# An encoder trunk whose input projection goes from 256 to 512 columns a step

## The chip, the cores and the metric

The kernel runs on one core of a Trainium2 chip. The metric is the device time of the whole program in microseconds (us): the median of three runs was 1551.15 us (1551.09 to 1554.43). All inputs and outputs are float32 in the chip's main memory.

## The reference, cut to what matters

There are two layers over 1024 tokens of width 1024. Each layer normalises its input, projects it with one weight matrix of 1024 x 3072, runs three groups of attention heads side by side, gates their outputs, projects them back and adds a normalised result to its input.

```python
for l in range(2):
    proj = rms_norm(x, pre_norm[l]) @ w_in[l]            # 1024 x 3072
    dq, dk, dv, dgate, gq, gk, gv, ggate, mq, mgate = split(proj,
        [384, 384, 384, 384, 384, 128, 128, 384, 256, 256])
    # 6 differential heads: (softmax(q1 k1) - lam * softmax(q2 k2)) v, rotary on q, k
    oa = rms_norm(diff_attention(rope(dq), rope(dk), dv, lam), subln) * silu(dgate)
    # 6 grouped-query heads on 2 kv heads, q and k normalised, axial rotary
    ob = gqa(axial(rms_norm(gq)), axial(rms_norm(gk)), gv) * silu(ggate)
    # 4 heads over 256 memory tokens
    mk, mv = split(rms_norm(mem, mem_norm[l]) @ w_mem_kv[l], 2)
    om = softmax(mq mk / 8) mv * silu(mgate)
    x = x + rms_norm(concat(oa, ob, om) @ w_out[l], post_norm[l])
```

## The kernel before, in words

**Precision.** Projections and scores are computed from float32 values split in two: a high half that TensorE takes in one pass and the rest as a low half. A product needs three matmuls (high x high, high x low, low x high). Line 493 issues them for the input projection, line 1394 for the output projection. For the products with the values, ScalarE writes the exponential (line 853) and its half-precision copy `eh` (line 857), GpSimd or VectorE the rest `el` (line 860), and lines 504 to 506 multiply both with the values.

**Input projection.** The 3072 columns are cut into 12 chunks of 256 (`dq0`, `dk0`, ... ; some join two pieces of 128 from different places), and the memory projection into two (`mk`, `mv`). For a chunk and a tile of 128 tokens, a *step* runs 8 blocks of rows x 3 products = 24 matmuls into half of a PSUM bank (`matmul_chunk`). Its weights come as four pieces of 256 rows x 256 columns (`load_piece`): a DMA into one of three raw buffers `rt`, the high half by ScalarE (line 392), the low half by VectorE or GpSimd (line 393 or 394), into one of eight places of the ring `wt`. A place is free again once the last tile's step has used it. After a step `post` takes the result out of PSUM: rotary and normalisation on VectorE and GpSimd (`rope_lin`, `rope_ax`), transposes on TensorE (line 662) and a store to a scratch tensor for query and key columns (`put_T`), a split of values (`put_v`), a tanh for gates (`put_gate`).

**Stages of a layer.** Chunks `dq0`, `dk0`, `dv0`, `mk`, `mv` run first, in PSUM tiles of two banks (kinds `s0`, `s1`). The nine others run in single banks (kind `st`) as filler of low priority beside differential attention: 12 half-heads, each of 16 maximum matmuls (line 1026, reduced by line 897) and eight units of scores (line 1036), each unit with its exponential. Every two units make one product with the values (`pv_part`). Then come the grouped-query heads (lines 1238, 1239, 1250, 1251) and the memory heads (1293, 1294), then the output projection and the norms, in which the next layer's input is normalised and its first weights are loaded.

**Order of the work.** Nothing is ordered by hand. A planner (`Plan`) simulates five engines, the DMA queue, PSUM banks (`Banks`, with a priority and a limit for each kind in `KINDS`) and rings of buffers, with a cost for each operation (`PE`, `ACT`, `DVE`, `POOL`, `LAT`), and every engine's instructions are issued in the order in which the plan starts them. All DMAs go through SP's queue. On the chip each queue then runs in that order, and waits where something is late.

Of the kernel before, what the change touches and what calls it, by code (L numbers as in the profile page):

```python
# [22 lines left out]
P = 128  # L23
# [11 lines left out]
DQ, DK, DV, DG, GQ, GK, GV, GG, MQ, MG = 0, 384, 768, 1152, 1536, 1920, 2048, 2176, 2560, 2816  # L35
CHUNKS = {
    "dq0": ((DQ, 256),),
    "dq1": ((DQ + 256, 128), (GK, 128)),
    "dk0": ((DK, 256),),
    "dk1": ((DK + 256, 128), (GV, 128)),  # L40
    "dv0": ((DV, 256),),
    "dv1": ((DV + 256, 128), (MQ, 128)),
    "dg0": ((DG, 256),),
    "dg1": ((DG + 256, 128), (MG, 128)),
    "gq0": ((GQ, 256),),
    "gq1": ((GQ + 256, 128), (MQ + 128, 128)),
    "gg0": ((GG, 256),),
    "gg1": ((GG + 256, 128), (MG + 128, 128)),
    "mk": ((0, 256),),
    "mv": ((256, 256),),  # L50
}
VCOLS = {"dv0": (0, 256), "dv1": (0, 128), "dk1": (128, 256), "mv": (0, 256)}
VKEY = {"dv0": "d0", "dv1": "d1", "dk1": "g", "mv": "m"}
# [21 lines left out]
DVE_FIX = 0.13  # L75
PV_N = 2
X_GATE, XT = 2, 4
DMA_RATE = 300.0
SLACK = 0.8

KINDS = {'un': (0.5, 2, 2), 'z': (1, 2, 2), 's0': (2, 2, 2), 's1': (0, 2, 2), 'st': (1, 4, 1), 'pv': (1, 1, 1), 'tr': (-1, 2, 1), 'mx': (2, 4, 1), 'zh': (3, 2, 1)}
# [6 lines left out]
class Event:  # L88
# [4 lines left out]
    def fire(self, plan):  # L93
        self.n -= 1
        if self.n == 0:
            for p in self.waiters:
                plan.push(plan.t, p, None)
            self.waiters = []

# [78 lines left out]
class Plan:  # L178
# [5 lines left out]
    def __init__(self):  # L184
        self.t = 0.0
        self.seq = 0
        self.heap = []
        self.busy = {k: False for k in self.LAT}
        self.queue = {k: [] for k in self.LAT}
        self.used = {k: 0.0 for k in self.LAT}  # L190
        self.until = {k: 0.0 for k in self.LAT}
        self.port = {"dve": 0.0, "pool": 0.0}
        self.live = 0
# [12 lines left out]
    def start(self, eng):  # L206
# [4 lines left out]
        self.used[eng] += dur  # L211
        if port:
            dur += max(0.0, self.port["pool" if eng == "dve" else "dve"] - self.t)
            self.port[eng] = self.t + dur
# [4 lines left out]
        self.push(self.t + dur + (self.LAT[eng] if lat is None else lat), proc, None)  # L219

    def advance(self, proc, val):
        gen, done = proc
        while True:
# [18 lines left out]
            if kind == "wait":  # L242
                if cmd[1].n > 0:
                    cmd[1].waiters.append(proc)
                    return
# [26 lines left out]
def trunk(ctx, tc, t_in, t_out):  # L272
# [80 lines left out]
    def pair(name, nb, n=S):  # L353
        return [dram.tile([P, nb, n], F32, name=f"{name}{i}") for i in range(2)]

    scr = {"dq0": pair("s_dqa", 2), "dq1": pair("s_dqb", 2), "dk0": pair("s_dka", 2), "dk1": pair("s_dkb", 1),
           "gq0": pair("s_gqa", 2), "gq1": pair("s_gqb", 2), "dv1": pair("s_mqa", 1), "mk": pair("s_mka", 2, NM)}


    def load_piece(src, j, cols, w, col, vmax, prio=0):  # L360

        ri = yield take("rt")
        rt = wr.tile([P, 2, NC], F32, name="rt")
        lst, off = [], 0
        for c0, n in cols:
            lst.append((rt[:, :, off:off + n],
                        src[j * 2 * P:(j + 1) * 2 * P, c0:c0 + n].rearrange("(a p) n -> p a n", p=P), n))
            off += n
        yield wait(dmas(lst, prio))
        if vmax is not None:  # L370
            v0, v1 = VCOLS[col]
            yield DVE(2 * (v1 - v0), lambda: dve.tensor_reduce(
                out=vmax[:, 1 + j:2 + j], in_=rt[:, :, v0:v1], axis=AX.XY, op=ALU.max, apply_absolute_value=True))
        hi, lo, wi = yield from split_w(rt)
# [4 lines left out]
    def split_w(rt, p2=None, name=None):  # L379
        if p2 == "big":  # L380
            wi = yield take("big")
            t = new_big()
            hi, lo = (t[:, h * 512:(h + 1) * 512].rearrange("p (a n) -> p a n", a=2) for h in range(2))
        elif p2 is None:
            wi = yield take("wt")
            hi = wp.tile([P, 2, NC], F32R, name="wt")
            lo = wp.tile([P, 2, NC], F32R, name="wt")
        else:
            wi = None
            hi = p2.tile([P, 2, NC], F32R, name=name + "h")  # L390
            lo = p2.tile([P, 2, NC], F32R, name=name + "l")
# [5 lines left out]
    def new_w():  # L397
        return {"t": [None] * 4, "ev": [Event() for _ in range(4)], "scale": Event()}

    def vscale(vmax, gmx, w, sc, key):  # L400
# [4 lines left out]
        yield DVE(4, lambda: dve.tensor_reduce(out=wm[:, 0:1], in_=vmax[:, 1:5], axis=AX.X, op=ALU.max))  # L405
# [77 lines left out]
    def matmul_chunk(ps, xhi, xlo, w, last, prio):  # L483

        for j in range(4):
# [14 lines left out]
    def attend(o, v, es):  # L500

        n = len(es)
        for kt, (eh, el) in enumerate(es):
            pe.matmul(o[:, 0:65], lhsT=eh, rhs=v[:, kt, 0:65], start=(kt == 0), stop=False, skip_group_check=True)  # L504
            pe.matmul(o[:, 0:64], lhsT=eh, rhs=v[:, kt, 66:130], start=False, stop=False, skip_group_check=True)  # L505
            pe.matmul(o[:, 0:65], lhsT=el, rhs=v[:, kt, 0:65], start=False, stop=(kt == n - 1),  # L506
                      skip_group_check=True)
# [4 lines left out]
    def make_layer(l):  # L512
# [4 lines left out]
        L.W = {c: new_w() for c in (*FIRST, *REST)}  # L517
# [5 lines left out]
        stored = {c: Event(NT if c != "mk" else 2) for c in scr}  # L523
        gate_ev = {c: Event(NT // 2) for c in ("dg0", "dg1", "gg0", "gg1")}
        vfull = {c: Event(NT if c != "mv" else 2) for c in VCOLS}
# [6 lines left out]
        opened = Event()  # L532
        attn_open = Event()


        def weights(chunks):
            for c in chunks:
                src = t_in["w_mem_kv"][l] if c in ("mk", "mv") else w_in
                vmax = None
                if c in VCOLS:  # L540
                    vmax = small.tile([P, 8], F32, name="gm")
                    pl.spawn(vscale(vmax, (lambda: mgm[0]) if c == "mv" else (lambda: L.gmx), L.W[c], sc, VKEY[c]))
                evs = []
                for j in range(4):
                    ev = Event()
                    pl.spawn(load_piece(src, j, CHUNKS[c], L.W[c], c, vmax, -7 if c == FIRST[0] else 0), ev)
                    evs.append(ev)
                yield wait(evs[1])
# [42 lines left out]
        def put_v(vt, ps, c, n, key):  # L591
# [3 lines left out]
            cv = sc[VKEY[c]]  # L595
# [4 lines left out]
            vfull[c].fire(pl)  # L600
# [55 lines left out]
        def put_T(nat, nb, c, t, ni):  # L656
# [3 lines left out]
            def f():  # L660
                for j in range(nb):
# [11 lines left out]
            yield wait(dmas([(scr[c][x][:, :nb, t * P:(t + 1) * P], raw(s)[:, :nb, :], 64 * nb)  # L673
                             for x, s in ((0, hi), (1, lo))]))
# [5 lines left out]
        def put_gate(ps, t, c, freed):  # L680
            k = yield take("sq")
            th = Q["pj"].tile([P, NC], F32, name="sq", bufs=SQ)
            yield ACT(NC, lambda: act.activation(th, ps, AF.Tanh, scale=0.5), POST, "p")
# [1107 lines left out]
```

## Time and profile before

| | |
|---|---|
| median of three runs | 1551.15 us |
| profiled execution, its own time | 1553.02 us |
| its span, first to last instruction | 1551.2 us |
| mean granted TensorE clock | 0.987 |
| TensorE busy, matmuls | 1487.1 us, 15920 instructions |
| VectorE, ScalarE, GpSimd busy | 1036.2, 896.5, 903.0 us |
| moved by DMA | 163.97 MB |

The span is what the profile covers; the execution's own time is 1.8 us longer. Busy time of TensorE includes the modelled tails of matmuls, which overlap; the mean of one matmul is for that reason longer than the distance from one to the next. A share of busy time is a mean over stages, so the tables of stages and the chain of waits are read beside it.

### The profile page before, as it was taken

The page shows a single profiled execution, that of the slowest core. Times are in us where ns is not written, and L with a number is a line of the kernel's source. Part 1 is how long each engine was busy: PE and PEld are TensorE (multiplying, and loading weights), DVE is VectorE, ACT ScalarE, POOL GpSimd, SP SyncE. Part 2 cuts the span into 40 slices and gives each one's busy share as a digit, 9 for nine tenths or more (in the row PEclk, how much of TensorE's full clock was granted, in tenths as well). Part 3 has the DMA queues.
Part 4 walks back from the last instruction along what each step waited for, and adds up shares of the span by engine and source line. Part 5 has one row for each costly group of instructions (what it writes and reads, how often), then busy time and mean ns, then how long its engine had stood idle before and what let it go on. Part 6 is the DMA issues. An engine that isn't in the chain of part 4 may idle for free. (4 is left out here: it accounts for less than half of the span.)

```text
span 1551.2 us, 39344 instructions
## 1 busy us (share of the span) xinstructions
PE 1487.1 (96%) x15920; PEld 1375.1 (89%) x15920; DVE 1036.2 (67%) x2042; ACT 896.5 (58%) x1428; POOL 903.0 (58%) x647
## 2 busy tenths in 40 slices
PE   6999999999999999999999999999999998899997
PEld 5999999989999888888889999999899998788886
DVE  7747776788865886825566487776887757777143
ACT  4332668767668576673333346677657657576511
POOL 4133668789768486561122257678887757585500
PEclk9999999999999998999999999999999999899999
DMA  6435223233323644215254523223332156332242
GB/s 203 134 106 152 77 77 103 71 96 94 95 82 84 175 117 100 57 49 199 94 163 133 137 83 97 80 59 103 111 104 63 56 144 174 79 84 70 83 147 95
DMA packets 166048, 163.97 MB, mean 106 GB/s; under 512 B 14853, under 2 KB 140357, under 8 KB 165866
## 3 DMA queue, kind: packets, MB, share of 16 engines
q1 hardware_dynamic: 165866, 161.46, 35.7%
q8 instruction: 125, 2.05, 0.6%
q14 instruction: 57, 0.47, 0.1%
HBM read 110.96 MB, written 50.09 MB: 104 GB/s over the span
## 5 line engine op out<-in xcount | busy, mean ns | idle before, releaser
L860 POOL TENSOR_TENSOR el<-e,eh 128x1024 f16<-128x1024 f32 x258 | 570.0, 2221 | 208.0 <-ACT eh L857 194.7
L897 DVE TENSOR_REDUCE mx<-ps 128x1 f32<-128x512 f32 (+1 forms) x608 | 404.6, 684 | 145.6 <-PE ps L1026 86.8
L493 PE MATMUL ps<-wt,big 128*128 128x256 f32 x3456 | 490.0, 285 | 2.0 <-DVE nat L606 1.7
L493 PEld LDWEIGHTS ps<-wt,big 128*128 128x128 f32 x3456 | 465.0, 190 | 18.8 <-ACT e L853 2.0
L853 ACT ACTIVATE e<-pp 128x1024 f32<-128x1024 f32 x304 | 309.3, 1024 | 108.2 <-PE pp L1251 61.9
L857 ACT ACTIVATE eh<-e 128x1024 f16<-128x1024 f32 x262 | 275.4, 1057 | 2.4
L504 PEld LDWEIGHTS <-eh 128*128 128x128 f16 x2144 | 195.0, 96 | 14.4 <-issue 10.9
L394 POOL TENSOR_TENSOR wt<-rt,wt 128x512 fp32r<-128x512 f32 x89 | 123.7, 1401 | 136.6 <-ACT wt L392 96.0
L506 PEld LDWEIGHTS <-el 128*128 128x128 f16 x2144 | 196.6, 99 | 3.8 <-POOL el L860 3.4
L505 PEld LDWEIGHTS <-eh 128*128 128x128 f16 x2144 | 196.6, 97 | 0.7 <-issue 0.5
L436 POOL TENSOR_SCALAR u<-ss 128x1 f32<-128x1 f32 (+3 forms) x96 | 23.9, 249 | 253.3 <-DVE ss L1478 109.0
L493 PE MATMUL pp<-wt,big 128*128 128x256 f32 x1152 | 156.5, 291 | 8.8 <-POOL wt L394 4.1
L1026 PE MATMUL ps<-sdk,sdq 96*128 96x512 f32 x384 | 158.2, 413 | 3.9 <-DVE mx L897 2.4
L493 PEld LDWEIGHTS pp<-wt,big 128*128 128x128 f32 x1152 | 144.6, 194 | 11.7 <-POOL wt L394 4.9
L504 PE MATMUL ps<-vd,eh 128*128 128x65 f16 x1536 | 150.3, 193 | 0.2
L505 PE MATMUL ps<-vd,eh 128*128 128x64 f16 x1536 | 149.5, 194 | 0.0
L506 PE MATMUL ps<-vd,el 128*128 128x65 f16 x1536 | 149.0, 192 | 0.0
L1036 PE MATMUL pp<-sdq,sdk 98*128 98x256 f32 x768 | 125.8, 286 | 0.0
L1036 PEld LDWEIGHTS pp<-sdq,sdk 98*128 98x128 f32 x768 | 112.5, 190 | 5.3
L1250 PE MATMUL pp<-big 128*128 128x256 f32 x384 | 102.6, 297 | 0.3 <-ACT e L853 0.3
L1251 PE MATMUL pp<-big 67*128 67x256 f32 x384 | 100.3, 291 | 1.5 <-DMA big<-nl 1.5
L949 ACT ACTIVATE o<-ps 128x130 f32<-128x130 f32 (+1 forms) x160 | 46.1, 288 | 92.7 <-PE ps L506 91.8
(243 smaller groups left out, 2829.4 us busy)
## 6 DMA issues: line engine op xcount, KB each, us to landing
rt<-in_w_in SPq DMA_DIRECT2D x48, 256.0 KB
rt<-in_w_in SPq DMA_DIRECT2D x96, 128.0 KB
gt<-g_scr SPq DMA_DIRECT2D x32, 256.0 KB
rt<-in_w_out SPq DMA_DIRECT2D x32, 256.0 KB
sdq<-s_dqa SPq DMA_DIRECT2D x48, 128.0 KB
sdk<-s_dka SPq DMA_DIRECT2D x48, 128.0 KB
big<-s_gqa SPq DMA_DIRECT2D x24, 256.0 KB
big<-s_gqb SPq DMA_DIRECT2D x24, 256.0 KB
```

What stands on the lines that cost most here:

```text
L394: (POOL(512, lambda: pool.tensor_sub(out=lo, in0=rt, in1=raw(hi))), W_BIAS[1]))
L493: pe.matmul(ps, lhsT=x[:, kt, :], rhs=y[:, a, :], start=(kt == 0 and n == 0), stop=(kt == KT - 1 and n == 2))
L504: pe.matmul(o[:, 0:65], lhsT=eh, rhs=v[:, kt, 0:65], start=(kt == 0), stop=False, skip_group_check=True)
L505: pe.matmul(o[:, 0:64], lhsT=eh, rhs=v[:, kt, 66:130], start=False, stop=False, skip_group_check=True)
L506: pe.matmul(o[:, 0:65], lhsT=el, rhs=v[:, kt, 0:65], start=False, stop=(kt == n - 1), skip_group_check=True)
L853: yield ACT(1024, lambda: act.activation(e, ps, AF.Exp, scale=scale), 0, "p")
L857: yield either((ACT(1024, lambda: act.activation(eh, e, AF.Copy)), 0.0), (DVE(1024, lambda: dve.tensor_copy(out=eh, in_=e), 0, fast=True, ...
L860: (POOL(1024, lambda: pool.tensor_sub(out=el, in0=e, in1=eh)), 0.0))
L897: yield DVE(512, lambda: dve.tensor_reduce(out=out_ap, in_=src, axis=AX.X, op=ALU.max), MXP[0])
L1026: yield (512, lambda ps, n=n: pe.matmul(ps, lhsT=q()[0:96, i * P:(i + 1) * P], rhs=k()[0:96, n * 512:(n + 1) * 512], start=True, stop=True ...
L1036: pe.matmul(ps[:, a * 256:(a + 1) * 256], lhsT=k()[0:98, kt * P:(kt + 1) * P], rhs=q()[0:98, j * 256:(j + 1) * 256], start=True, stop=True)
L1250: pe.matmul(o, lhsT=ka()[:, ks], rhs=a()[:, qs], start=True, stop=False)
```

## The change

The 12 chunks become six blocks A to F of 512 contiguous columns, and the two memory chunks become one block M. A step runs 24 matmuls of 512 columns into a whole bank. A piece of weights is now 128 rows x 512 columns, of the same size, and a block has eight. The ring keeps its eight places; six of M's pieces go to a memory pool of its own. Block A runs alone first, then B, C, D, F and E as filler and M beside them; a count of finished units limits how early a filler step may start. What is taken out of PSUM after a step is grouped anew, and scratch tensors are one for each of q, k and so on. A product with the values is issued in two steps: all high parts once the high halves are there, the low parts once the low halves are. The planner's costs get new figures and a model of TensorE's clock.

```diff
-CHUNKS = { "dq0": ((DQ, 256),), "dq1": ((DQ + 256, 128), (GK, 128)),
...
-FIRST = ("dq0", "dk0", "dv0", "mk", "mv")
-REST = ('dg0', 'dq1', 'dk1', 'dv1', 'gq1', 'gq0', 'dg1', 'gg1', 'gg0')
-W_SLOTS = 8
+BLOCKS = {"A": 0, "B": 512, "C": 1024, "D": 1536, "E": 2048, "F": 2560, "M": 0}
+FIRST = ("A",)
+REST = ("B", "C", "D", "F", "E")
+ORDER = ("A", "B", "M", "C", "D", "F", "E")
+W_SLOTS, MP_HOME = 8, 6
-DVE_FIX = 0.13
-PV_N = 2
-X_GATE, XT = 2, 4
+DVE_FIX = 0.08
+LEAD, PER_STEP = 18, 4
+PV_AT, PVL = 0, 0.1
+X_GATE, XT = 3, 4
+PE_RATE, CLOCK_WINDOW, CLOCK_LOW, CLOCK_HIGH = 2175.0, 3.41, 0.33, 0.85
-KINDS = {... 'st': (1, 4, 1), ...}
+KINDS = {... 'st': (1, 3, 1), ...}
...
+    def clocked(self, dur):
+        while self.window < int(self.t / CLOCK_WINDOW):
+            share = self.work / CLOCK_WINDOW
+            self.half = share < (CLOCK_HIGH if self.half else CLOCK_LOW)
+            self.window += 1
+            self.work = max(0.0, self.work - CLOCK_WINDOW)
+        dur *= 2.0 if self.half else 1.0
+        self.work += dur
+        return dur
...
     def PE(ncols, fn, prio=0, lat=None):
-        return use("pe", ncols / 2210.0, fn, prio, lat)
+        return use("pe", ncols / PE_RATE, fn, prio, lat)
     def ACT(n, fn, prio=0, src="s"):
-        return use("act", (0.2 if src == "s" else 0.17) + n / 1200.0, fn, prio)
+        return use("act", (0.095 if src == "s" else 0.05) + n / 1200.0, fn, prio)
...
     def matmul_chunk(ps, xhi, xlo, w, last, prio):
-        for j in range(4):
+        for j in range(KT):
             yield wait(w["ev"][j])
             hi, lo, wi = w["t"][j]
             def f(j=j, hi=hi, lo=lo):
-                for a in range(2):
-                    kt = 2 * j + a
-                    for n, (x, y) in enumerate(((xhi, hi), (xhi, lo), (xlo, hi))):
-                        pe.matmul(ps, lhsT=x[:, kt, :], rhs=y[:, a, :], start=(kt == 0 and n == 0),
-                                  stop=(kt == KT - 1 and n == 2))
-            yield PE(6 * NC, f, prio, None if j == 3 else 0.0)
+                for n, (x, y) in enumerate(((xhi, hi), (xhi, lo), (xlo, hi))):
+                    pe.matmul(ps, lhsT=x[:, j, :], rhs=y, start=(j == 0 and n == 0), stop=(j == KT - 1 and n == 2))
+            yield PE(3 * NB_COLS * 0.98, f, prio, None if j == KT - 1 else 0.0)
             if last and wi is not None:
                 free("wt", wi)
...
         def weights(chunks):
...
-                yield wait(evs[1])
+                if c == "M":
+                    yield wait(mp_open)
+                for j in range(KT):
+                    home = (lambda: Q["mp"]) if c == "M" and j < MP_HOME else None
+                    pl.spawn(load_piece(src, j, BLOCKS[c], L.W[c], VCOLS.get(c), vmax, ..., home), ev)
+                yield wait(evs[KT - 3])
...
+            if c == "A":
+                return freed, [heads(a, NC, (("dq", 0, 2, 0),), "A0", t, lin_all, freed),
+                               heads(b, NC, (("dq", 2, 1, 0), ("dk", 0, 1, 1)), "A1", t, lin_all, freed)]
...
+        def steps(blocks, kind, prio):
+            two = KINDS[kind][2] == 2
+            k = -LEAD
...
+                    if kind == "st":
+                        yield "count", d_units_done, PER_STEP * k
+                        k += 1
+                    if not two or t % 2 == 0:
+                        slot = yield take_ps(kind)
...
         def exp_part(ps, slot, scale, kind, box, ev, n32):
...
+            box.append((eh, el, ei))
+            ev[0].fire(pl)
             yield either((DVE(1024, lambda: dve.tensor_sub(out=el, in0=e, in1=eh), ...
             free("e32", n32[1])
-            box.append((eh, el, ei))
-            ev.fire(pl)
+            ev[1].fire(pl)
...
         def pv_part(it, u, es, evs, prev, mine):
             for e in evs:
-                yield wait(e)
+                yield wait(e[PV_AT])
...
-            yield PE(sum(c for _, c in some) + 100, lambda: [f() for f, _ in some], PVP)
+            yield PE(sum(c for _, c in some) * 2 / 3 + 50, lambda: [f(0) for f, _ in some], PVP, 0.0)
+            for e in evs:
+                yield wait(e[1])
+            yield PE(sum(c for _, c in some) / 3 + 50, lambda: [f(1) for f, _ in some], PVL)
...
-            first = Event(2)
-            pl.spawn(steps(FIRST[:1], "s0", 1), first)
-            pl.spawn(steps(FIRST[1:2], "s1", 1.1), first)
-            yield wait(first)
-            yield from steps(FIRST[2:], "s0", 1)
+            yield from steps(FIRST, "s0", 1)
+            pl.spawn(steps(("M",), "s1", 0.4))
             pl.spawn(steps(REST, "st", STP))
```

## Rows read from the trace of the kernel before

**Rows 1.** The page, part 1: busy us, share of the span, instructions.
```profile
PE 1487.1 (96%) x15920; PEld 1375.1 (89%) x15920; DVE 1036.2 (67%) x2042; ACT 896.5 (58%) x1428; POOL 903.0 (58%) x647
```

**Rows 2.** Table of stages: length, busy us (instructions) by engine, clock, DMA, GB/s.
```profile
0.00:25.00 25.00, 13.14 (x59) 9.95 (x60) 14.78 (x18) 13.11 (x23) 10.97 (x22) 1.00 0.63 209
75.00:100.00 25.00, 23.32 (x180) 22.61 (x180) 13.91 (x32) 9.49 (x19) 11.04 (x10) 0.93 0.41 122
300.00:400.00 100.00, 97.95 (x1223) 93.68 (x1222) 77.92 (x178) 69.40 (x115) 92.05 (x82) 1.00 0.39 110
525.00:600.00 75.00, 69.08 (x788) 61.51 (x788) 62.11 (x83) 55.57 (x75) 54.49 (x28) 0.93 0.43 116
...
150.00:525.00 375.00, 369.39 (x4528) 352.65 (x4527) 277.25 (x612) 249.84 (x392) 278.10 (x199) 1.00 0.33 93
525.00:700.00 175.00, 166.24 (x2056) 146.22 (x2056) 117.68 (x171) 125.39 (x169) 122.73 (x59) 0.97 0.33 90
890.00:1250.00 360.00, 352.98 (x4279) 337.30 (x4278) 269.40 (x600) 239.73 (x380) 269.14 (x194) 1.00 0.31 89
1280.00:1450.00 170.00, 159.71 (x1901) 141.30 (x1899) 118.54 (x175) 120.68 (x160) 116.53 (x57) 0.95 0.35 92
```

**Rows 3.** Groups of TensorE by form: count, busy us, mean ns, idle before.
```profile
L493 PE MATMUL ps<-wt,big 128*128 128x256 f32 x3456 | 490.0, 285 | 2.0 <-DVE nat L606 1.7
L493 PE MATMUL pp<-wt,big 128*128 128x256 f32 x1152 | 156.5, 291 | 8.8 <-POOL wt L394 4.1 <-DVE nat L606 4.0 <-ACT wt L392 0.6
L493 PE MATMUL pp<-wt,mh 128*128 128x256 f32 x128 | 23.9, 286 | 0.0
L493 PE MATMUL pp<-wt,ml 128*128 128x256 f32 x64 | 18.0, 282 | 0.0
```

**Rows 4.** The chain that ended last, in order: start us, us, piece.
```profile
1182.67 2.86 PE ps L493 x24
...
1239.08 1.44 PE ps L493 x12
1242.47 2.23 PE ps L493 x18
...
1271.44 0.72 PE ps L493 x6
...
1432.60 1.39 PE ps L1394 x6
...
1481.45 9.54 PE pp L1394 x42
...
1503.07 11.60 PE pp L1394 x51
...
1517.63 19.17 PE pp L1394 x85
```

**Rows 5.** Timeline 774 to 792 us, first and last of eight splits of weights.
```profile
774.25 0.63 ACT L392 ACTIVATE wt<-rt 128x512 fp32r<-128x512 f32 x1 [0.50 <-PE pp L1394]
...
789.35 2.54 POOL L394 TENSOR_TENSOR wt<-rt,wt 128x512 fp32r<-128x512 f32 x2 [1.39 <-ACT wt L392]
```

**Rows 6.** Timeline 82 to 85 us: TensorE waits for weights of the third chunk.
```profile
82.69 0.39 PE L493 MATMUL pp<-wt,big 128*128 128x256 f32 x1 [0.56 <-ACT wt L392]
...
84.21 0.90 PE L493 MATMUL pp<-wt,big 128*128 128x256 f32 x5 [1.13 <-POOL wt L394]
```

**Rows 7.** Timeline of the first 34 us: projection matmuls, and the eighth piece.
```profile
16.97 2.91 PE L493 MATMUL pp<-wt,big 128*128 128x256 f32 x12
...
20.21 1.67 PE L493 MATMUL pp<-wt,big 128*128 128x256 f32 x12
...
23.44 3.12 PE L493 MATMUL pp<-wt,big 128*128 128x256 f32 x24
...
26.75 1.68 PE L493 MATMUL pp<-wt,big 128*128 128x256 f32 x12
...
31.48 1.26 POOL L394 TENSOR_TENSOR wt<-rt,wt 128x512 fp32r<-128x512 f32 x1
```

**Rows 8.** Waits of TensorE: us in total, times, longest.
```profile
PE ps L506 <- POOL elm L860: 6.5, 7, 1.8
PE pp L493 <- POOL wt L394: 4.1, 4, 1.6
PE pp L493 <- DVE nat L606: 4.0, 6, 1.2
PE ps L506 <- POOL el L860: 3.2, 2, 1.6
...
PE ps L493 <- DVE nat L606: 1.7, 2, 0.8
...
PE ps L662 <- DVE nat L606: 1.4, 1, 1.4
```

**Rows 9.** Timeline 203 to 204 us: rotary of 128 columns on VectorE.
```profile
203.21 0.29 DVE L614 TENSOR_TENSOR rb<-ps,lin 128x128 f32<-128x128 f32 x1 [0.22 <-ACT vg L596]
203.42 0.29 DVE L614 TENSOR_TENSOR ps<-ps,lin 128x128 f32<-128x128 f32 x1
203.81 0.22 DVE L605 TENSOR_TENSOR nat<-ps,rb 128x64 f32<-128x64 f32 x1
203.96 0.21 DVE L606 TENSOR_TENSOR nat<-ps,rb 128x64 f32<-128x64 f32 x1
```

More of the change, by code (lines that the diff above doesn't have):

```diff
@@ L98, in fire, with __init__, add @@
             self.waiters = []
+class Count:
+    def __init__(self):
+        self.n = 0
+        self.waiters = []
+    def add(self, plan):
+        self.n += 1
+        rest = []
+        for n, p in self.waiters:
+            if n <= self.n:
+                plan.push(plan.t, p, None)
+            else:
+                rest.append((n, p))
+        self.waiters = rest
 class Ring:
@@ L192, in __init__ @@
         self.port = {"dve": 0.0, "pool": 0.0}
+        self.window, self.work, self.half = 0, 0.0, False
         self.live = 0
@@ L244, in advance @@
                     cmd[1].waiters.append(proc)
+                    return
+            elif kind == "count":
+                if cmd[1].n < cmd[2]:
+                    cmd[1].waiters.append((cmd[2], proc))
                     return
@@ L397, in new_w @@
     def new_w():
[L398 removed]
+        return {"t": [None] * KT, "ev": [Event() for _ in range(KT)], "scale": Event()}
     def vscale(vmax, gmx, w, sc, key):
@@ new lines, in plain, with heads @@
+        def plain(o, s, n, freed):
+            yield ACT(n, lambda: act.activation(o, s, AF.Copy), POST, "p")
+            freed.fire(pl)
+        def heads(ps, n, dests, key, t, how, freed):
+            ni = yield take("nat")
+            nat = Q["pj"].tile([P, NC], F32, name="nat", bufs=NAT)[:, 0:n]
+            parts = how(nat, ps)
+            done = Event(len(parts))
+            for g in parts:
+                pl.spawn(g, done)
+            yield wait(done)
+            yield from put_T(nat, n // P, dests, key, t, ni)
@@ L758, in post @@
+        def post(c, t, ps, rid):
+            freed, parts = parts_of(c, t, ps)
             done = Event(len(parts))
@@ L798, in make_layer @@
-        pend = Event((len(FIRST) + len(REST) - 2) * NT + 4)
+            rid()
+            yield wait(done)
+        def steps(blocks, kind, prio):
+            two = KINDS[kind][2] == 2
+            k = -LEAD
+            yield wait(opened)
+            slot, held = None, None
+            for c in blocks:
+                n = 2 if c == "M" else NT
+                for t in range(n):
+                    if c == "M":
+                        yield wait(mem_ready[t])
+                        hi, lo = mT[t]
+                    else:
+                        yield wait(L.xT_ev[t])
+                        hi, lo = L.xT[t]
+                    yield wait(L.W[c]["ev"][0])
+                    if kind == "st":
[3 more added lines that the diff above has]
+                        slot = yield take_ps(kind)
+                        held = Event(2 if two else 1)
+                        pl.spawn(give_back(slot, held))
+                    h = t % 2 if two else 0
+                    ps = slot[3][:, h * NB_COLS:(h + 1) * NB_COLS]
+                    yield from matmul_chunk(ps, hi, lo, L.W[c], t == n - 1, prio)
+                    if c == REST[-1]:
+                        if t == 0:
+                            rest_on.fire(pl)
+                        for s in L.xT_slot[t]:
+                            free("big", s)
+                    if c == "M" and t == 1:
+                        close_pool(pools["mp"])
+                        open_attn()
+                    pl.spawn(post(c, t, ps, lambda held=held: held.fire(pl)), pend)
@@ L992, in pv_list @@
                     es.append((eh[:, o:o + P], el[:, o:o + P]))
-                out.append((lambda c=66 * i, es=es: attend(ps[:, c:c + 65], v, es), 201 * nk))
+                out.append((lambda low, c=66 * i, es=es: attend(
+                    ps[:, c:c + 65], v, [e[low] for e in es], low, c == 0), 198 * nk))
             return out
@@ L1179, in open_gm @@
             yield wait(rest_on)
-            for c in scr:
-                if c in ("dq1", "mk"):
-                    yield wait(stored[c])
+            for c in ("D1", "mk"):
+                yield wait(stored[c])
             for key in GKEYS:
@@ L1557, in begin @@
         def begin():
-            yield from weights((*FIRST, *REST))
+            yield from weights(ORDER)
         def main(nxt):
```

292 lines of the change are left out of this document (117 added, 175 removed).

## The prediction

> **What bounds the kernel now.** I read four views in this order. First the page's busy times: TensorE is busy for 1487.1 of 1551.2 us, VectorE for 67% and ScalarE and GpSimd for 58% [rows 1]. A busy TensorE includes modelled tails, so the second view is the table of stages. In the long stretch of layer 1 in which differential attention runs beside the projection (150 to 525 us) TensorE is busy for 369.39 of 375 us at full granted clock; VectorE, ScalarE and GpSimd stand at 277, 250 and 278 us, some 74, 67 and 74%. The same stretch of layer 2 (890 to 1250) looks alike, the grouped-query stretches (525 to 700, 1280 to 1450) are at 95 and 94%, and only the first 25 us have TensorE idle for half of the time [rows 2]. So TensorE sets the time nearly everywhere, and what is taken off it shows in the span unless a new wait takes its place.
>
> Third, the groups of TensorE's work: line 493, the input projection, has 3456 + 1152 + 128 + 64 = 4800 matmuls of 256 columns [rows 3]. Their mean of 285 ns is no pace, since matmuls overlap. The pace is read in the fourth view, the chain that ended last: 24 of them in 2.86 us, 12 in 1.44, 6 in 0.72, that is 0.119 to 0.120 us each. So the projection costs 4800 x 0.120 = 576 us, 37% of the span. The same chain holds line 1394, the output projection, with the same kind of operands (float32r halves from the same ring, three products an element pair) at 512 columns: 42 in 9.54 us, 51 in 11.60, 85 in 19.17, that is 0.226 to 0.227 us each [rows 4].
>
> **The change part by part.**
>
> *Width 512 (the main term).* 4800 matmuls of 256 become 2400 of 512, for the same columns. Each pair goes from 2 x 0.120 = 0.240 to 0.227 us, 0.013 saved; 2400 x 0.013 = 31 us less. Ends: short groups of line 1394 in the chain run at 1.39 / 6 = 0.232, which leaves 0.240 - 0.232 = 0.008, 19 us; groups of line 493 broken by other work run at 2.23 / 18 = 0.124, and 0.248 - 0.226 gives 0.022, 53 us [rows 4]. I take 31 because long groups of both widths agree among themselves. It counts in full: line 493 stands in the chain itself, and no stage that holds it leaves TensorE idle for more than a few per cent [rows 2].
>
> The rows put 0.012 to 0.014 us on each matmul beyond its columns (0.120 x 2 - 0.227). The Trainium skill (TensorE: Matmul & The Clock Gate, Back-to-back issue gap) states N / 2.4 + 2.5 ns for a warm isolated matmul, 109 ns at 256 columns and 216 at 512; a pair would then give back only 2.5 ns, an estimate of 6 us for 2400. The measured 120 and 227 ns disagree with it in just the part that this change saves, and I go by them.
>
> *Weights: one block fills the ring.* The ring of split weights has eight places before and after. A chunk of 256 columns took four, so the next chunk was loaded while one ran; a block of 512 takes all eight, so the next block's first piece can be split only as the last step of the old block lets a place go. How long eight pieces take is seen where layer 2 begins: the first split starts at 774.25, the last is done at 789.35 + 2.54 = 791.89, 17.6 us for eight [rows 5], with three raw buffers ahead of the ring and its places coming free one by one, as they will. With T the start of a block's last step, a place comes free at T + 0.7 (three matmuls), the eighth piece is ready at T + 18.3, and the next block's first step ends at T + 19. Unhindered it would end at T + 2 x 24 x 0.227 = T + 10.9: a gap of 8 us where nothing else stands. Within attention the new count lets one step start for every four units; 96 units in 375 us make 15.6 us a step, longer than the gap, so boundaries C-D, D-F and F-E are covered by pace, with attention matmuls beside them. Block M (two steps, 10.9 us, six of eight pieces in places of its own) covers B-C. What is left is A-B, once a layer: 8 us less some 1 us of transposes that are due there, 7. The kernel before pays there too: TensorE waited 0.56 and 1.13 us for weights at 82 to 84 us [rows 6], about 2 us with what the clock lost (0.93 in that stage, [rows 2]). Net 2 x (7 - 2) = 10 us more. Ends: 0 if the memory tiles' transposes fill it, 25 if both gaps are whole and the clock then falls to its half level (1.2 GHz) for ten microseconds, as long as the fall about 583 us that the 0.93 of 525 to 600 us shows (2 x (8 + 5)).
>
> *Start of a layer.* The first step now needs eight pieces (2 MB) where it needed four. Before, the eighth piece of the start is done at 31.48 + 1.26 = 32.7 us, and by then TensorE had finished three steps of 256 columns [rows 7]; a changed kernel with that load has finished one of 512, two old ones, 3 us behind. But it now fetches those pieces ahead of x tiles 2 to 7 instead of among them. In layer 2 the eighth piece is there at 791.89, when the old kernel had run two steps as well. I take 0, ends -3 and +6.
>
> *Products with the values in two parts.* The high parts now start when the high halves are there, and the low third follows when the low halves are. The same 2432 x 3 matmuls run. TensorE waited 6.5 + 3.2 us for low halves (line 506) [rows 8], nine times, 1.1 us each; two thirds of a product can now run in that time. I take -4, somewhat under half, since the low part can still be reached too early; ends -9.7 (all of it) and +5 (half as much again, for the further place in each product at which TensorE's queue can stop; behind it stand scores and projection steps).
>
> *Work after a step.* Rotary parts of 256, 256, 128 and 128 columns become three of 256, four gates become three; stores of rotated heads go from 14 to 16 a tile on SP's queue, stores of gates from six to three for two tiles. That takes four VectorE instructions of 0.29, 0.29, 0.22 and 0.21 us a tile away [rows 9], 16 us of VectorE in all, beside a TensorE that is busier. I take 0; if VectorE is late it gives at most its waits, 4.0 + 1.7 + 1.4 us on the rotated tile [rows 8]: ends -7 and 0. A bank is now held for a step of 5.4 instead of 2.9 us, with the same number of bytes used up per column; 0.
>
> *The plan's figures and the pacing.* Every engine's order is written out by the planner, so new figures move everything a little. Nothing prices this but the idle time: at best it gives back TensorE's 1551.2 - 1487.1 = 64 us [rows 1], at worst it adds as much as both grouped-query stretches idle now, (175 - 166.24) + (170 - 159.71) = 19 us [rows 2]. I take 0.
>
> **Sum.** -31 + 10 + 0 - 4 + 0 + 0 = -25 us on the profiled run's 1553.02, which is 1528. The median of the runs shown is 1551.15, 1.9 lower; so 1526.
>
> **Rivals.**
> *Slower: the refill is not covered.* Place: the ring of eight, five boundaries a layer, ten in all. A whole gap costs 8 us and some 2 of clock. It decides against the change once the mean gap over the ten is above (31 + 4) / 10 = 3.5 us. With A-B whole (2 x 10) and the other eight at 4, less the 2 x 2 paid now: 20 + 32 - 4 = 48, against 35: +13, 1564. For it: eight pieces take 17.6 us, and waits for weights exist even with two chunks in the ring [rows 5, 6]. Against: pacing of one step in 15.6 us, and block M's own places. 0.11.
>
> *No gain in attention.* The other engines take over there, so only blocks A, B and M count: 2 x 18 x 24 x 0.013 = 11 us, less 4, plus 10: -5, 1546. For it: GpSimd is busy for 92.05 of 300 to 400 us. Against: TensorE is at 97.95 in the same stage, and GpSimd's share can go to VectorE (77.92) [rows 2]. 0.13.
>
> *A much better order.* Half of the 64 idle microseconds go too: -25 - 32, 1494. For it: short waits are spread over many lines [rows 8], which is what a plan that is off by a tenth of a microsecond makes. Against: they sum to little, and the largest idle stretch is the start, which no order mends. 0.14.
>
> *The forecast*, 1526, own range 1510 to 1544: 0.62.
>
> What a measurement of this kernel can tell from no change is 0.3%, 4.7 us, so faster means below 1546.5. Faster: 0.61 of the forecast, 0.05 of the second rival, 0.14 of the third, 0.80. Within: 0.01 + 0.07 + 0.02 = 0.10. Slower: 0.01 of the second and 0.09 of the first, 0.10. The range reaches from the third rival to just short of no change, 1494 to 1549: it takes in the 53 us end of the main term and, upward, the 25 of the refill against 31.
>
> **What would show it.** Right: the projection's chain rows at 0.226 to 0.232 us a matmul and 2400 of them; a wait of TensorE for weights of 5 to 8 us between A and B in each layer, and nearly none at other boundaries; fewer microseconds on line 506's successor; the attention stretches still at 98% TensorE. Wrong: a pace above 0.235, waits for weights at many boundaries, or a TensorE share below 95% in 150 to 500 us with ScalarE or GpSimd near 90%, which would mean that another engine has taken over. If the time is far below 1510, the order has done it, not the width.

## The result and the profile after

The changed kernel takes 1590.45 us (median of four runs, 1589.22 to 1599.58), the kernel before, run beside it, 1552.79: a ratio of 1.0253 (95% interval 1.0210 to 1.0296), slower by some 38 us. The forecast was 1526 and its range ended at 1549, so time and sign are both wrong. The profiled span is 1587.4 us, 36.2 more than before. The mean granted clock of TensorE is 0.986, before 0.987, so a lower clock does not explain the 36 us.

The page's part 1 of the kernel after, against [rows 1], and its groups of the projection (line 512 now), against [rows 3]. The last columns of a group are busy us, mean ns, and the idle time before it with what ended it:

```profile
PE 1500.8 (95%) x13520; PEld 1238.1 (78%) x13520; DVE 1069.7 (67%) x1996; ACT 878.8 (55%) x1373; POOL 851.4 (54%) x620
...
L512 PE MATMUL ps<-wt,big 128*128 128x512 f32 x1920 | 532.0, 403 | 13.0 <-DVE sl L701 4.8
L512 PE MATMUL pp<-wt,big 128*128 128x512 f32 x384 | 105.0, 417 | 19.1 <-DVE nat L636 19.1
```

The 2400 matmuls fewer are there (13520 against 15920), yet TensorE's busy time did not fall. The second group, block A in its two-bank tiles, has an idle time that it did not have: 19.1 us, all of it ended by VectorE's rotary (line 636, `nat`).

TensorE's waits of the kernel after (us in total, times, longest), against [rows 8]:

```profile
PE pp L512 <- DVE nat L636: 19.1, 16, 1.5
...
PE ps L692 <- DVE nat L636: 6.2, 13, 0.5
PE ps L512 <- DVE sl L701: 4.8, 4, 1.6
PE ps L512 <- POOL wt L415: 4.5, 5, 1.1
...
PE ps L512 <- ACT wt L413: 3.0, 4, 1.4
...
PE ps L524 <- POOL el L909: 2.2, 2, 1.1
```

The first row was 4.0 us in six waits. The wait for low halves (line 506 before, 524 now) went from 9.7 to 2.4 us (0.2 of it in a row not shown), as the split of the products should make it.

The table of stages of the kernel after, against [rows 2] (length, then busy us and count of TensorE, its weight loads, VectorE, ScalarE, GpSimd, the granted clock, DMA):

```profile
75.00:100.00 25.00, 19.76 (x88) 14.36 (x88) 17.11 (x48) 10.99 (x24) 13.76 (x12) 0.93 0.55 158
300.00:400.00 100.00, 97.98 (x1039) 79.97 (x1039) 71.70 (x154) 68.76 (x106) 80.61 (x61) 0.98 0.35 100
...
150.00:525.00 375.00, 367.65 (x3674) 304.41 (x3673) 269.73 (x552) 245.43 (x366) 273.57 (x195) 0.99 0.32 91
```

The attention stretch is as full as before (367.65 of 375 us), so no other engine took over there. What is lost at once lies ahead of it: from 75 to 100 us TensorE is busy for 19.76 us, before for 23.32.

The timeline of the kernel after inside block A (start, us, engine, line, operation, count, and in brackets the idle time before it and its releaser):

```profile
72.74 2.45 PE L512 MATMUL pp<-wt,big 128*128 128x512 f32 x10
...
75.22 0.42 DVE L644 TENSOR_TENSOR rb<-pp,lin 128x256 f32<-128x256 f32 x1 [1.79 <-PE pp L512]
...
75.57 0.42 DVE L644 TENSOR_TENSOR pp<-pp,lin 128x256 f32<-128x256 f32 x1
76.02 0.29 DVE L635 TENSOR_TENSOR nat<-pp,rb 128x128 f32<-128x128 f32 x1
76.23 0.28 DVE L636 TENSOR_TENSOR nat<-pp,rb 128x128 f32<-128x128 f32 x1
...
76.56 1.66 PE L512 MATMUL pp<-wt,big 128*128 128x512 f32 x6 [1.38 <-DVE nat L636]
...
78.26 0.42 DVE L644 TENSOR_TENSOR rb<-pp,lin 128x256 f32<-128x256 f32 x1 [1.75 <-PE pp L512]
...
79.69 1.62 PE L512 MATMUL pp<-wt,big 128*128 128x512 f32 x6 [1.47 <-DVE nat L636]
```

This is two engines taking turns. VectorE's rotary of a finished step starts only when TensorE's matmuls already issued for the next step are done (75.19), and TensorE's next matmul starts only when that rotary is done (76.51). Neither works while the other does, though the two steps lie in two banks: what they share is the tile. All 16 waits stand in the second step of such a pair, and 14 of them inside it, after 3, 6 or 12 of its 24 matmuls, so they are not waits for a free bank. Two successive steps of a two-bank kind now use one tile, a bank each (`if not two or t % 2 == 0` in the diff); before, each step took a tile of its own. The rotary rewrites its half in place (line 644, `pp` from `pp`), and the program puts waits between accesses to one tile (argued here from the rows; e1 and e5 try it).

The Trainium skill (PSUM — Partial Sum Buffer, PSUM bank collisions raise a hardware error) says that two engines must not be on the same bank, in the same partitions, at once and that accesses to different banks ran clean. By that rule nothing in the chip asks for these waits; the first experiment agrees, since there the steps lie in different banks too and the waits are gone.

### The profile page after: what moved, and what is told of

Same layout as the page of the kernel before. It is cut to its first block, busy times and chain, and to the rows that moved or that the text cites. A ratio compares the mean times of both kernels' runs of the same rounds, so it can differ in the third digit from the quotient of the medians.

```text
span 1587.4 us, 34133 instructions
## 1 busy us (share of the span) xinstructions
PE 1500.8 (95%) x13520; PEld 1238.1 (78%) x13520; DVE 1069.7 (67%) x1996; ACT 878.8 (55%) x1373; POOL 851.4 (54%) x620
## 5 line engine op out<-in xcount | busy, mean ns | idle before, releaser
L512 PE MATMUL ps<-wt,big 128*128 128x512 f32 x1920 | 532.0, 403 | 13.0 <-DVE sl L701 4.8
L512 PEld LDWEIGHTS ps<-wt,big 128*128 128x128 f32 x1920 | 349.6, 190 | 84.3 <-POOL wt L415 7.1
L415 POOL TENSOR_TENSOR wt<-rt,wt 128x512 fp32r<-128x512 f32 x72 | 99.5, 1391 | 135.4 <-ACT wt L413 68.2
L527 PEld LDWEIGHTS <-eh 128*128 128x128 f16 x2176 | 143.1, 99 | 26.1 <-issue 20.8
L457 POOL TENSOR_SCALAR u<-ss 128x1 f32<-128x1 f32 (+3 forms) x96 | 21.7, 226 | 256.7 <-DVE ss L1527 112.8
L529 PEld LDWEIGHTS <-eh 128*128 128x128 f16 x2176 | 144.7, 98 | 6.5 <-issue 6.4
L512 PE MATMUL pp<-wt,big 128*128 128x512 f32 x384 | 105.0, 417 | 19.1 <-DVE nat L636 19.1
L527 PE MATMUL ps<-vd,eh 128*128 128x65 f16 x1536 | 112.0, 195 | 3.2 <-DVE mx L945 3.0
L529 PE MATMUL ps<-vd,eh 128*128 128x64 f16 x1536 | 111.0, 194 | 0.0
L512 PEld LDWEIGHTS pp<-wt,big 128*128 128x128 f32 x384 | 71.4, 197 | 37.0 <-DVE nat L636 22.3
L524 PEld LDWEIGHTS <-el 128*128 128x128 f16 x2176 | 74.7, 98 | 22.8 <-issue 13.9
L700 ACT ACTIVATE sh<-ps 128x256 fp32r<-128x256 f32 x100 | 38.5, 385 | 93.0 <-PE ps L692 85.8
```

What stands on the lines that cost most here:

```text
L415: (POOL(512, lambda: pool.tensor_sub(out=lo, in0=rt, in1=raw(hi))), W_BIAS[1]))
L512: pe.matmul(ps, lhsT=x[:, j, :], rhs=y, start=(j == 0 and n == 0), stop=(j == KT - 1 and n == 2))
L527: pe.matmul(o[:, 0:65], lhsT=e, rhs=v[:, kt, 0:65], start=(first and kt == 0), stop=False, skip_group_check=True)
L529: pe.matmul(o[:, 0:64], lhsT=e, rhs=v[:, kt, 66:130], start=False, stop=False, skip_group_check=True)
```

## The experiments

Each ratio is to the kernel before, run beside it (medians 1552.64 to 1554.91). Two times worked out from the traces are used throughout. The distance from the start of one matmul to the start of the next is compared with its pace (120 ns for 256 columns, 227 for 512, and so for each kind). What it has beyond the pace is a *stall* where this excess is over 140 ns, and *short excess* where it is under 140 ns. Before has 81.2 us of stalls and 65.9 of short excess, after 118.8 and 95.7. With the pairs at 227 instead of 240 ns (2400 x 13 = -31.2) this makes -31.2 + 37.6 + 29.8 = 36.2, the whole difference of the spans. The split has a weakness: in stretches at the half clock (1.2 GHz) the median distances are 427 and 213 ns, so that there a matmul of 512 columns, 200 ns over its pace, counts as a stall, and one of 256, 93 ns over, as short excess.

**e1, a tile for each step.** The changed kernel; each step of blocks A and M takes a two-bank tile and uses one bank of it.

```diff
-            two = KINDS[kind][2] == 2
+            two = False
```

> The changed kernel, but each step of blocks A and M takes a two-bank PSUM tile of its own and uses its first bank, as the kernel before did, instead of two steps sharing one tile. Theory 1 (shared tile): VectorE's rotary, which reads and rewrites one half of the tile, is ordered against TensorE's writing of the other half, and that is the 19.1 us that TensorE waits for nat in block A (16 times); these waits should fall below 5 us and the time to 1566 to 1576. Rival (VectorE is late in block A by its own load, as it norms x and rotates): the same waits stand before the next step's first matmul, and the time stays within 4 us of 1590.

Measured: 1564.69 us (1561.64 to 1567.22), ratio 1.0064 (1.0041 to 1.0087). The waits in block A are gone. Timeline of this kernel at the same place, and its first waits:

```profile
71.89 3.02 PE L512 MATMUL ps<-wt,big 128*128 128x512 f32 x12
```

```profile
71.98 0.41 DVE L644 TENSOR_TENSOR rb<-pp,lin 128x256 f32<-128x256 f32 x1
72.31 0.42 DVE L644 TENSOR_TENSOR pp<-pp,lin 128x256 f32<-128x256 f32 x1
```

```profile
PE ps L477 <- DVE xt L497: 8.3, 3, 5.0
PE ps L692 <- DVE nat L636: 6.2, 13, 0.5
PE ps L512 <- POOL wt L415: 5.8, 8, 1.1
```

The rotary now runs at 71.98 beside TensorE's matmuls. Block B's first matmuls (`ps` at line 512) start at 71.89 us; in the kernel after they start here, in layer 1 and in layer 2:

```profile
83.33 2.98 PE L512 MATMUL ps<-wt,big 128*128 128x512 f32 x12
...
870.28 2.21 PE L512 MATMUL ps<-wt,big 128*128 128x512 f32 x9
```

That is 11.4 us later in layer 1. In layer 2 e1 has them at 843.75, so the kernel after is 26.5 us behind by then, as much as the spans differ in all (26.0). The time is 1 us below what theory 1 had forecast, and the rival, within 4 us of 1590, is out. So some 26 of the 38 us come from the shared tile (29 by the two ratios). One row stays: transposes waiting for the same rotary, 6.2 us in 13 waits.

**e5, the same sharing put into the kernel before.** Two successive steps of 256 columns in its two-bank kinds share a tile, in different banks.

```diff
...
-                slot = yield take_ps(kind)
-                ps = slot[3][:, 0:NC]
+                two = KINDS[kind][2] == 2
+                if not two or t % 2 == 0:
+                    slot = yield take_ps(kind)
+                    held = Event(2 if two else 1)
+                    pl.spawn(give_back(slot, held))
+                h = t % 2 if two else 0
+                ps = slot[3][:, h * 512:h * 512 + NC]
...
```

> The kernel before (256 columns, old figures, products in one step) with one thing taken from the change: two successive steps of the chunks that run in two-bank tiles (dq0, dk0, dv0, mk, mv) share one tile, each in a bank of its own. Theory 1 (shared tile) expects TensorE to wait for nat in lines of pp in the middle of the next step, 12 us or more beside the 4.0 of before, and 1564 to 1580. Rival (the waits of block A come from 512 columns, whose rotary is twice as long, not from sharing): within 5 us of 1553.

Measured: 1578.86 us, ratio 1.0150 (1.0120 to 1.0179). Its waits:

```profile
PE ps L506 <- POOL el L870: 10.9, 12, 2.2
...
PE pp L493 <- DVE nat L606: 7.6, 11, 1.4
PE ps L506 <- DVE el L869: 7.2, 4, 3.1
PE pp L493 <- DVE vd L597: 6.3, 7, 1.1
...
PE ps L506 <- DVE elm L869: 3.2, 2, 1.6
```

Sharing alone makes the kernel before slower. The waits at it are 7.6 + 6.3 us where [rows 8] have 4.0; but those for low halves rose too, from 9.7 to 21.3 us (10.9 + 7.2 + 3.2), which are not waits at the tile; the order that the plan made anew is the likely reason, not shown. At the tile there are 3.6 us more for the rotary and 6.3 for line 597, which takes values out and only reads the tile: rewriting in place is not needed for such a wait. Together that is 9.9 us more, under the 12 of the forecast, so it was in part luck that the time fell into the range of 1564 to 1580. So this run supports the mechanism and does not give its price; e1 does.

**e6, values after the rotary in block B.** In B one bank holds key columns (rotary, VectorE) and value columns (taken out by ScalarE, then VectorE). The kernel after has the rotary wait:

```profile
118.65 0.47 ACT L625 ACTIVATE vd<-ps,vc 128x256 f16<-128x256 f32 x1 [3.66 <-PE ps L512]
119.16 0.42 DVE L644 TENSOR_TENSOR rb<-ps,lin 128x256 f32<-128x256 f32 x1 [3.71 <-ACT vd L625]
...
120.50 0.44 PE L692 MATMUL ps<-ident,nat 128*128 128x128 f32 x2 [0.52 <-DVE nat L636]
```

These two read different columns of one bank, one after the other (118.65 + 0.47 = 119.12). That is a pair which the section of the Trainium skill cited above forbids at the same time. The plan did not know it: it started both at once and placed the transposes too early. e6 is e1 with the plan told, and with the two turned round: the rotary comes first.

```diff
+        def put_after(first, freed, vt, ps, c, n):
+            yield wait(first)
+            freed.fire(pl)
+            yield from put_v(vt, ps, c, n, freed)
...
-                               put_v(L.vd[:, 0:4], b, c, t, freed)]
+                               put_after(roped, freed, L.vd[:, 0:4], b, c, t)]
```

> As e1 (a tile for each step), and in block B the plan is told that ScalarE's reading of values follows VectorE's rotary in the same bank, which in e1 stand the other way round on the chip and make TensorE wait for nat before its transposes (13 times, 6.2 us). If unmodelled order on one PSUM bank is the general cause, these waits go and the time is 1556 to 1562; the rival (transposes wait for VectorE's load) expects no change from e1's 1565 beyond 3 us.

Measured: 1560.92 us, ratio 1.0031 (1.0011 to 1.0050); transposes wait 0.4 us for that rotary, before 6.2. This is inside the theory's range and just outside the rival's. Some 4 us, and the intervals of e1 and e6 overlap, so its size is uncertain, and whether the telling or the turning round did it was not separated. Waits of the kinds that the trace lists are now 52.3 us in all; before has 54.3.

**e9, the width undone in place.** e6 with each 512-column matmul issued as two of 256 into the two halves of the bank: same tiles, ring and order of steps.

```diff
-                    pe.matmul(ps, lhsT=x[:, j, :], rhs=y, ...
+                    for c in (0, 256):
+                        pe.matmul(ps[:, c:c + 256], lhsT=x[:, j, :], rhs=y[:, c:c + 256], ...
```

> e6 with one thing undone in place: each 512-column matmul of the input projection is issued as two of 256 columns, one behind the other, into the two halves of the same bank, so that order, tiles, ring and figures stay as in e6 (1560.9). It takes away the width and nothing else. Theory: the width gives what the start-to-start times show, 2 x 0.120 against 0.2317 us a matmul, 2400 x 0.0083 = 20 us, so 1578 to 1584 here. By the prediction's own term (0.013 a matmul) it gives 31, so 1590 to 1594. Rival: TensorE is not what bounds the attention stretches any more, so the width gives little, 1558 to 1568.

Measured: 1578.67 us, ratio 1.0171 (1.0144 to 1.0199). Against e6 this is 17.8 us by the medians, 21.7 by the two ratios (0.0140 x 1553): the width is worth some 20 us, as its theory had it, not 31, and not nothing. The spans of the two profiled executions lie only 14.0 us apart, for e9's ran at a granted clock of 0.990 and e6's at 0.985; by TensorE's starts outside the stretches at the half clock the projection of e9 takes 20.7 us more. The chain of waits of three kernels shows why (start, us, piece): first e9, then e6, then the kernel after.

```profile
87.90 2.87 PE ps L513 x24
...
103.49 5.76 PE ps L513 x48
```

```profile
57.19 5.46 PE pp L512 x24
...
102.16 5.50 PE ps L512 x24
...
180.17 2.15 PE ps L512 x9
```

```profile
1231.04 0.70 PE ps L512 x3
1231.84 1.40 PE ps L512 x6
...
1296.06 2.10 PE ps L512 x9
```

Of 256 columns, 48 take 5.76 us, 0.120 each. Of 512, 24 in a row take 5.46 to 5.50, 0.228 to 0.229, but three, six or nine in a row mostly take 0.230 to 0.245 each (0.70 / 3 and 2.10 / 9 are 0.233, 2.15 / 9 is 0.239), and beside attention the plan issues them by threes. The median distance of all 2400 is 233 ns: (240 - 233) x 2400 = 17 us.

The Trainium skill (TensorE: Matmul & The Clock Gate, Back-to-back issue gap) gives 109 ns for an isolated matmul of 256 columns, 216 for 512, and 131 as measured in a stream of 512-column ones. No row here shows any of the three: these are 120 and 228 to 245 ns.

**e3, the split products alone**, in the kernel before.

```diff
-            yield PE(sum(c for _, c in some) + 100, lambda: [f() for f, _ in some], PVP)
+            yield PE(sum(c for _, c in some) * 2 / 3 + 50, lambda: [f(0) for f, _ in some], PVP, 0.0)
+            for e in evs:
+                yield wait(e[1])
+            yield PE(sum(c for _, c in some) / 3 + 50, lambda: [f(1) for f, _ in some], PVL)
...
```

> The kernel before with only the products with the values in two steps. If more places at which TensorE's queue can stop are what costs, slower than 1552 by 10 us or more. If the split is what it was priced at, 1540 to 1552.

Measured: 1556.37 us, ratio 1.0014 (0.9995 to 1.0033): no change. It lies in neither range of the forecast, nearer to the second. Two things cancel in its trace. Stalls fall from 81.2 to 67.2 us, while the short excess rises from 65.9 to 82.3, of which 7.3 is behind the products themselves and 6.0 behind the projection.

**e7, the split undone in e1.** One step again, with the high parts of a product issued first and its low parts behind them.

```diff
-PV_AT, PVL = 0, 0.1
+PV_AT, PVL = 1, 0.1
...
-            yield PE(sum(c for _, c in some) * 2 / 3 + 50, lambda: [f(0) for f, _ in some], PVP, 0.0)
...
-            yield PE(sum(c for _, c in some) / 3 + 50, lambda: [f(1) for f, _ in some], PVL)
+            yield PE(sum(c for _, c in some) + 100, lambda: [f(x) for x in (0, 1) for f, _ in some], PVP)
```

> As e1, with products with the values in one step. Split products run at 32 ns where 29 was the pace, in e3 too, where fewer waits made that good. If that holds here: 1560 to 1570. If the split costs in this structure: under 1558.

Measured: 1564.29 us, ratio 1.0064 (1.0044 to 1.0085), the same as e1. The split is worth nothing that these runs can tell in either kernel.

**e4, the plan's figures alone**, in the kernel before: the new costs and the clock model, nothing else (in full also the new costs of ScalarE, of a product, of scores and of a step of the output projection).

```diff
-DVE_FIX = 0.13
+DVE_FIX = 0.08
...
+PE_RATE, CLOCK_WINDOW, CLOCK_LOW, CLOCK_HIGH = 2175.0, 3.41, 0.33, 0.85
...
```

> The kernel before with only the planner's new figures and clock model. If an order made with these figures is what costs 38 us, 1575 or more. If the blocks cost it, within 10 us of 1552.

Measured: 1569.81 us, ratio 1.0096 (1.0074 to 1.0119). That is between the two forecasts: the order costs the kernel before some 15 us, not 38. A good part of it is the clock, which was granted at 0.979 in the profiled execution and at 0.987 in that of the kernel before: by TensorE's starts, stretches at the half clock hold 29.1 us beyond the pace, before 17.2, and the span is 18.6 us longer.

**e8, the old figures in e1**: the old costs of TensorE's rate, VectorE and ScalarE, and no clock model. The new costs of a product, of scores and of a step of either projection stay.

```diff
-DVE_FIX = 0.08
+DVE_FIX = 0.13
...
-PE_RATE, CLOCK_WINDOW, CLOCK_LOW, CLOCK_HIGH = 2175.0, 3.41, 0.33, 0.85
+PE_RATE, CLOCK_WINDOW, CLOCK_LOW, CLOCK_HIGH = 2210.0, 3.41, -1.0, -1.0
...
```

> As e1, with the planner's old figures and no clock model. The new figures cost the kernel before 15 us (e4). If they cost here too, 1545 to 1555; if they were fitted to these blocks and carry them, 1575 or more.

Measured: 1624.39 us, ratio 1.0449 (1.0421 to 1.0476), 60 us above e1. Its waits:

```profile
PE ps L527 <- ACT eh L904: 11.2, 12, 1.6
...
PE ps L524 <- POOL el L909: 10.6, 10, 1.8
```

Much the same figures cost the kernel before 15 us and save the new blocks 60. They are good or bad only with the work that they order: with the old ones, products come before the halves of their exponentials are there. That is 21.8 us of the waits shown. Another large part is the clock, granted at 0.971 here and at 0.987 in e1: stretches at the half clock hold 44.8 us beyond the pace against 16.2. That the waits brought the clock down was not tried by itself.

**e2, the width without the split and with the old figures**, from the changed kernel, so with the shared tile; it also has the old costs of products, of scores and of the output projection.

```diff
-PV_AT, PVL = 0, 0.1
+PV_AT, PVL = 1, 0.1
...
-PE_RATE, CLOCK_WINDOW, CLOCK_LOW, CLOCK_HIGH = 2175.0, 3.41, 0.33, 0.85
+PE_RATE, CLOCK_WINDOW, CLOCK_LOW, CLOCK_HIGH = 2210.0, 3.41, -1.0, -1.0
...
-            yield PE(3 * NB_COLS * 0.98, f, prio, None if j == KT - 1 else 0.0)
+            yield PE(3 * NB_COLS, f, prio, None if j == KT - 1 else 0.0)
...
```

> The changed kernel with products with the values in one step again and the planner's old figures (no clock model): blocks of 512, their PSUM tiles, ring and order alone. If the loss is in the blocks (shared tile, one block fills the ring, later start of attention), it is at least as slow as the changed kernel, 1585 or more. If the loss is in the new figures or in the split products, it is between 1530 and 1560.

Measured: 1611.11 us, ratio 1.0370 (1.0339 to 1.0401), as forecast for a loss in the blocks; but old figures alone give e1 60 us (e8), so it does not show where the loss is. Wide blocks in an order made for other costs are slower than all four parts together. As a way to find what the width is worth this was a poor experiment, since the order moved with it; e9 is the clean one.

**e10, two costs set as measured**, in e6.

```diff
-            yield PE(3 * NB_COLS * 0.98, f, prio, None if j == KT - 1 else 0.0)
+            yield PE(3 * NB_COLS * 0.985, f, prio, None if j == KT - 1 else 0.0)
...
-                    ps[:, c:c + 65], v, [e[low] for e in es], low, c == 0), 198 * nk))
+                    ps[:, c:c + 65], v, [e[low] for e in es], low, c == 0), 209 * nk))
```

> e6 with the plan told two paces as the trace shows them: 0.985 instead of 0.98 of a step's nominal time for the projection, and 209 instead of 198 columns a key tile for the first part of a product with the values. Nothing of the work changes, only the order written out. If what is left against the kernel before (8 us) lies in a plan that is off by such amounts, it ends at 1545 to 1555; if orders merely scatter by a few us whatever they are told, at 1555 to 1567, with no side preferred.

Measured: 1555.85 us, ratio 1.0013 (1.0000 to 1.0026). By 1 us it lies on the side of orders that scatter, too near to the border (1555) to tell the two apart; stalls hardly moved (92.0 to 93.8 us). The 4.4 us between the spans of the two profiled executions (1559.4 and 1555.0) are no more than the clock gave, 0.985 in e6's and 0.990 in this one: 5.6 us less beyond the pace in stretches at the half clock. It is level with the kernel before; no version run here beats that.

## Why the prediction was wrong

**The step that failed is the last of "Work after a step"**: "A bank is now held for a step of 5.4 instead of 2.9 us, with the same number of bytes used up per column; 0." It counted bytes and banks, not which steps share a tile. The diff shown ahead has the line, and nothing was made of it. Measured: 16 waits, 19.1 us by the trace and some 26 us of time (e1), with some 4 more (e6, uncertain) for the bank that rotary and values share in B. The same part bounded VectorE's lateness at -7 to 0, taking the waits on the rotated tile as something only to be won. No rival named this place, and it alone turns e1's +0.6% into +2.5%.

**Width, -31: right in kind, a third too large.** The lower end, 19 us from short groups, is what came: 17.8 to 21.7 (e9). The choice of the value was the mistake. The prediction took the long groups "because long groups of both widths agree among themselves", though most steps run beside attention, in short ones. The count of 2400 came as written; of the pace forecast, 0.226 to 0.232, the long groups keep to it (0.228 to 0.229), and many short ones lie above it, up to 0.245.

**Weights, +10: too dear.** It named 5 to 8 us between A and B in each layer; the kernel after shows about 2 us in layer 1,

```profile
88.99 0.50 PE L512 MATMUL ps<-wt,big 128*128 128x512 f32 x1 [0.92 <-ACT wt L413]
90.61 0.73 PE L512 MATMUL ps<-wt,big 128*128 128x512 f32 x2 [1.12 <-POOL wt L415]
```

and 3.1 in layer 2 (0.85 + 1.43 + 0.85). All its waits for weights are 4.5 + 3.0 us, in the kernel before 4.1 + 0.6 [rows 3]: about 3 more, not 10. As stalls, from start to start, they are 10.1 against 5.9 us, 4 more, with 2.5 and 4.3 us at the two boundaries from A to B. (The upper end of the term, 2 x (8 + 5), is 26 and not 25.) That block A took longer does not explain it, for in e1, where it does not, they are 7.4 us (10.7 from start to start), as much. So the rival that ended slower, at 1564, is not what happened either.

**Split products, -4: nothing** (e3, whose interval leaves -1 to +5 us, and e7). The waits did fall (9.7 to 2.4 us), but products and the work behind them run a little slower, which the prediction had put only into its upper end, +5.

**Start of a layer, 0**: not measured by itself. The waits on normalised tokens (line 477, `xt` and `hn`) are 14.0 us in the kernel after, line 456's in the kernel before 8.9 (8.2 + 0.7), so it may hold up to 5 us. The "three steps" that TensorE had finished by 32.7 us are 67 matmuls, not quite 72.

**The plan's figures, 0**: as an effect of the figures alone wrong in size, +15 in the kernel before (e4, inside the bounds of -64 to +19) and about -60 in the new blocks (e8, with most of the figures). The term's bounds took idle time alone; what a new order does to the clock, some 12 us in e4 and 29 in e8, is not in them. They can't be priced apart from the blocks; 0 with such bounds was the fair entry, and e4 to e8 show that orders move this kernel by as much as any term of the sum. The pacing count is part of this and was not tried alone.

**What is left without the shared tile.** e6 stands 8.2 us of span above the kernel before (4.8 by the ratio), although the width gives some 20. By TensorE's starts: -31.2 of width at its long-group pace; +28.5 of short excess (15.3 behind the projection, most of it the short groups; 8.8 behind the products; 4.4 elsewhere); +10.8 of stalls, of which 9.2 are ahead of projection steps. About 5 of these 9.2 are no waits but matmuls of 512 columns at the half clock, counted as stalls where those of 256 are not. With the stretches at the half clock taken out, an estimate from the same starts reads -31.2, +31.0 of short excess (16.7 behind the projection, 7.4 behind the products, 6.9 elsewhere), +6.2 of stalls (4.5 ahead of the projection) and +2.1 inside those stretches. That is where the gain went; why products run slower is open (below), and so is the cause of the stalls that are left.

## What to carry to other kernels

Before a step is widened, list for each buffer who writes and who reads it while the next step runs: two steps in one tile, or two readers in one bank, are a new wait, whatever the bytes. Price a matmul by the length of the runs in which it will be issued, not by the longest run in the trace. And where a planner writes the order, test a part by changing it in place with the order kept, as in e9: a part taken out with a new order (e1, e2, e5) measures the order as well. For e1 the trace shows the waits that went and the start of each layer; e2 has no such row. Read the granted clock of such a run beside its waits: nearly half of what e8 lost against e1 stands in stretches at the half clock (28.6 of 61.0 us of span).

## What was not expected of the hardware

The distance of two float32 matmuls of 512 columns differs with the run that they are in: in the chain rows 0.228 us in runs of 24 and mostly 0.230 to 0.245 in runs of three to nine, where 256 columns keep 0.119 to 0.120 in many runs of 6, 12, 24 and 48 ([rows 4], e9). Short runs stand beside attention, long ones mostly do not, so the length and what runs beside it are not separated. The products with the values, some 65 columns of half precision, lie 30.6 ns apart on average in the kernel before and 31.8 after (distances under 80 ns). All that e3 and e7 show of it is that it comes with the high parts issued ahead of the low ones, also where both are one step: 7296 x 1.2 ns = 9 us. What in the new sequence makes it was not tried.
